# Block 2's attention: unscaled probabilities, and outputs divided by row sums that a transpose spreads

## The chip, the cores and the metric

One NeuronCore of a Trainium2 chip runs the whole program. The metric is the device time of one execution in microseconds (us); lower is better.

## What is computed

The program is two transformer blocks over 256 tokens of width 1024, in float32. Only the attention of block 2 is touched here. It has two kinds of eight heads each, head size 64: a windowed attention with a sink (kind 0, four query heads share a key head) and a neighbourhood attention with a bias (kind 1). Cut to what matters:

```python
s = concat([s_loc, s_ctx, sink_col], -1)     # kind 0; kind 1: concat([s_loc + bias, s_ctx], -1)
p = softmax(s, -1)
o = p_loc @ v_loc + p_ctx @ v_ctx            # 512 keys per query
merged = concat([rms_norm(o_a, g_a), rms_norm(o_b, g_b)], -1) @ w_out
x = x + g1 * merged
```

The gated feed-forward network (FFN) of block 2 follows on `x`.

## The kernel before

The attention works in 16 *units* (`typ`, `m`, `qt`): kind, pair of heads, half of the tokens (128 queries). Eight units of kind 0 come first, then eight of kind 1; here they are u0 to u15. Two units with the same `typ` and `m` (u0 and u1, u2 and u3, ...) make a *pair*. Four functions make up a unit:

- `scores` (L1605 to L1648): for each of the two heads, TensorE (PE) writes 128x512 scores into one PSUM bank (`sc`, tag `big`, 4 buffers). VectorE (DVE) takes the row maximum (L1621), or for kind 1 adds the bias and takes the maximum in one instruction (L1628); ScalarE (ACT) takes the exponential and sums it along the row (L1636); DVE forms the reciprocal of the two sums (L1640, 128x2); and the probabilities are scaled by it, the first head's on ACT (L1645), the second head's on DVE (L1647), as the table `NSC = ("AD",)` says.
- `turn` (L1650): PE transposes the probabilities in 128x128 pieces into PSUM (`ptp`, tag `tr`, 2 buffers); ACT copies one head's to SBUF, DVE the other's (`pT`, L1658).
- `outputs` (L1662): PE multiplies them with the values. The two heads' outputs lie in one tile with 64 rows each, transposed (rows are head dimensions, columns are queries): `po`, 128x256 for a pair, tag `mo`, one buffer.
- `finish` (L1673), once per pair: ACT squares `po` (`osq`, L1676), PE sums the squares down the rows (`psq`, tag `sm`, one buffer), DVE copies the sums (`ssab`, L1680), and ACT and DVE split `po` times the gain into a high and a low part (`moh` L1681, `mol` L1682). After a kind's fourth pair the rstd of the RMS norm is formed.

Then the output projection: 48 matmuls into four banks `pqa` (kind 0) and 48 into four banks `pqb` (kind 1), 128x512 each, in three terms (`moh`, `mol` with `wq..h`, `wq..l`). DVE evicts each bank with rstd and gate (`tmp` L1747, `tmpb` L1757) and POOL or DVE adds it to `x` (L1748, L1759, L1761). DVE also splits the weights (`wq0l` to `wq3l`, and `fg0l` for the FFN; L196), ACT makes their high parts (L189).

The code issues a unit's scores one unit ahead (`AHEAD = 1`) and a pair's `finish` after the next unit has begun (`LATE`). The order in which each engine really runs its instructions is not that of the code: the program is built with `schedule_with_timeline_sim=True`, which rearranges all of them ahead of time. At run time each engine takes its own list strictly in order and waits where an operand isn't there.

Of the kernel before, what the change touches and what calls it, by code (L numbers as in the profile page):

```python
# [12 lines left out]
AF = mybir.ActivationFunctionType  # L13
ALU = mybir.AluOpType
# [3 lines left out]
P = 128  # L18
# [91 lines left out]
def tile_kernel(ctx: ExitStack, tc: tile.TileContext, I, out, dbg=None):  # L110
    nc = tc.nc
    PE, ACT, DVE, POOL, SP = Ordered(tc, nc.tensor), nc.scalar, nc.vector, nc.gpsimd, nc.sync
# [20 lines left out]
    def at(shape, tag, name, bufs=1, dt=F32):  # L133
        return S_["act"].tile(shape, dt, tag=tag, name=name, bufs=bufs)
# [15 lines left out]
    def pt_(shape, tag, name):  # L150
        return S_["ps"].tile(shape, F32, tag=tag, name=name, bufs=S_["banks"][tag])

    def psm(shape, name, tag="sm"):
        return pso.tile(shape, F32, tag=tag, name=name)
# [62 lines left out]
    def rstd_of(ssq, n, mean, eps, name):  # L217

        v = tmp_([P, n], "rv", name + "v", bufs=4)
        DVE.tensor_scalar(v, ssq, mean, eps, op0=ALU.mult, op1=ALU.add)  # L220
        r = tmp_([P, n], "rs", name, bufs=4)
        S_["pow"] = POOL.tensor_tensor(r, v, mhalf[:, :n], op=ALU.pow)
        return r
# [58 lines left out]
    ident = cst[:, C_ID:C_ID + P]  # L282
# [441 lines left out]
    for tt in range(2):  # L724
        p = pt_([P, 4, P], "rec", "po")
# [73 lines left out]
    prs = {}  # L799
# [83 lines left out]
    for tt in range(2):  # L883
        ts = slice(tt * P, (tt + 1) * P)
        for i in range(2):
            p = pt_([P, 4, P], ("gu", "y")[tt], "pt")
# [406 lines left out]
    for u in range(8):  # L1293
# [85 lines left out]
        p = pt_([P, 256], "tr", "pst")  # L1379
# [163 lines left out]
    def proj_lat(c0, name):  # L1543
        hi, lo = latw[c0]
        if c0 in NEXT:
            n = NEXT[c0]
            latw[n] = split_w(kvw[n], "lat", pool=PLAT)
        p = pt_([P, 2, 256], "big", name + "p")
        for tt in range(2):
            ts = slice(tt * P, (tt + 1) * P)  # L1550
            for k in range(8):
                mm3(p[:, tt], hth[:, k, ts], htl[:, k, ts], hi[:, k], lo[:, k], k == 0, k == 7)
        return p
# [19 lines left out]
    for n, (c0, name, use) in enumerate(jobs):  # L1573
        if n == 3:
            after(ACT.activation(ready, mhalf[:, :1], AF.Exp), S_["hi"])
        p = proj_lat(c0, name)
# [25 lines left out]
    rab = []  # L1602
    ssab = at([P, 2, 2, 4], "ssab", "ssab")

    def scores(typ, m, qt):  # L1605

        q = (qa, qb)[typ]
        ts = slice(qt * P, (qt + 1) * P)
        t_ = at([P, 4, 2], "st", "st", bufs=4)
        scs = [pt_([P, 2, 256], "big", "sc2") for _ in range(2)]  # L1610
        for s in (1, 0):
            for s_ in range(2):
                kh, kl = (kAa[s][:, m // 2], kLa[s][:, m // 2]) if typ == 0 else (kAb[s][:, s_, m], kLb[s][:, s_, m])
                PE.matmul(scs[s_][:, s], lhsT=q[:, s_, m, ts], rhs=kh, start=True, stop=False)
                PE.matmul(scs[s_][:, s], lhsT=q[:, s_, m, ts], rhs=kl, start=False, stop=s + typ >= 1)
        prs = [at([P, 2, 256], "prb2", "prb2", bufs=NPR) for _ in range(2)]
        for s_ in range(2):
            sc = scs[s_]
            if typ == 0:
                PE.matmul(sc[:, 0, (1 - qt) * P:(2 - qt) * P], lhsT=identb, rhs=(maskc, maskn)[qt], start=False, stop=True)  # L1620
                DVE.tensor_reduce(t_[:, 0, s_:s_ + 1], sc, axis=AX.XY, op=ALU.max)  # L1621
            else:

                h = 2 * m + s_
                o = h % 4 * 384 + (2 - 2 * qt) * 64
                w = biasT[h][:, o:o + 256]
                w = bass.AP(tensor=w.tensor, offset=w.offset, ap=[w.ap[0], [1536 - o, 2], [1, 256]])
                DVE.tensor_tensor_reduce(prs[s_], sc, w, 1.0, NEG, ALU.add, ALU.max, t_[:, 0, s_:s_ + 1])  # L1628
        if typ == 0:
            DVE.scalar_tensor_tensor(t_[:, 0], t_[:, 0], -0.125, nsink[:, 2 * m:2 * m + 2], op0=ALU.mult, op1=ALU.min)  # L1630
            DVE.tensor_tensor(t_[:, 3], sinkB[:, 2 * m:2 * m + 2], t_[:, 0], op=ALU.add)
            ACT.activation(t_[:, 3], t_[:, 3], AF.Exp)
        else:
            DVE.tensor_scalar(t_[:, 0], t_[:, 0], -1.0, None, op0=ALU.mult)
        for s_ in range(2):
            S_["exp"] = ACT.activation(prs[s_], prs[s_] if typ else scs[s_], AF.Exp, bias=t_[:, 0, s_:s_ + 1],  # L1636
                                       scale=1.0 if typ else 0.125, accum_out=t_[:, 1, s_:s_ + 1])
        if typ == 0:
            DVE.tensor_tensor(t_[:, 1], t_[:, 1], t_[:, 3], op=ALU.add)
        DVE.reciprocal(t_[:, 2], t_[:, 1])  # L1640
        for s_ in range(2):
            r_ = t_[:, 2, s_:s_ + 1]
            e = NSC[(8 * typ + 2 * m + qt) % len(NSC)][s_]
            if e == "A":
                ACT.activation(prs[s_], prs[s_], AF.Copy, scale=r_)  # L1645
            else:
                (POOL if e == "P" else DVE).tensor_scalar(prs[s_], prs[s_], r_, None, op0=ALU.mult)  # L1647
        return prs,  # L1648

    def turn(prs):  # L1650
        pTs = []
        for s_ in range(2):
            pt = pt_([P, 4, P], "tr", "ptp")
            pf = prs[s_].rearrange("p s (a b) -> p (s a) b", b=P)
            for j in range(4):
                PE.transpose(pt[:, j], pf[:, j], ident)
            pT = at([P, 4, P], "pT2", "pT2", bufs=NPT)
            (DVE.tensor_copy if s_ else ACT.copy)(pT, pt)  # L1658
            pTs.append(pT)
        return pTs  # L1660

    def outputs(typ, m, qt, po_, pTs):  # L1662
        ts = slice(qt * P, (qt + 1) * P)
        for j in range(4):
            for s_ in range(2):
                h = 2 * m + s_
                if typ == 0:
                    v_ = va[j // 2][:, j % 2, (m // 2) * 64:(m // 2) * 64 + 64]
                else:
                    v_ = vb[j // 2][:, j % 2, h * 64:h * 64 + 64]  # L1670
                PE.matmul(po_[64 * s_:64 * s_ + 64, ts], lhsT=v_, rhs=pTs[s_][:, j], start=j == 0, stop=j == 3)

    def finish(typ, m, po_):  # L1673
        k = 4 * typ + m
        osq = at([P, 256], "mt", "osq2", bufs=3)
        ACT.activation(osq, po_, AF.Square)  # L1676
        psq = psm([P, 2], "psq")
        for tt in range(2):
            PE.matmul(psq[:, tt:tt + 1], lhsT=osq[:, tt * P:(tt + 1) * P], rhs=ones1, start=True, stop=True)
        DVE.tensor_copy(ssab[:, typ, :, m], psq)  # L1680
        ACT.activation(moh[:, k], po_, AF.Copy, scale=onT[:, k:k + 1])  # L1681
        DVE.scalar_tensor_tensor(mol[:, k], po_, onT[:, k:k + 1], moh[:, k], op0=ALU.mult, op1=ALU.subtract)  # L1682
        if m == 3:
            ssum = at([P, 2], "ssum", "ssum", bufs=2)
            DVE.tensor_reduce(ssum, ssab[:, typ], axis=AX.X, op=ALU.add)
            rab.append(rstd_of(ssum, 2, 1.0 / 512, EPS, f"rab{typ}"))
# [6 lines left out]

    units = [(typ, m, qt) for typ in range(2) for m in range(4) for qt in range(2)]
    ahead_ = [scores(*units[i]) for i in range(AHEAD)]
    late = []

    def hooks(i):

        nonlocal g1B  # L1700
        if i in G1U:
            g1B = row_bc(mod[:, 2, :, 0], kvc.tile([P, D], F32, tag="fB", name="g1B"))
        for h in BMU.get(i, ()):
            bias_mask(h)
        if i in WQU:
            w_blk2[WQU.index(i)] = w_block(WQU.index(i))
            after(S_["hi0"], S_["exp"])
# [4 lines left out]
    for i, un in enumerate(units):  # L1712
        pTs = turn(*ahead_.pop(0)) if AHEAD == 2 else None
        if late:
            finish(*late.pop())
        if i + AHEAD < len(units):
            ahead_.append(scores(*units[i + AHEAD]))
        pTs = pTs or turn(*ahead_.pop(0))
        if un[2] == 0:
            po_ = psm([P, 256], "po", "mo")  # L1720
        outputs(*un, po_, pTs)
        hooks(i)
        if un[2] == 1:
            late.append((*un[:2], po_))
            if not LATE:
                finish(*late.pop())
    PE.stop()
    if late:
        finish(*late.pop())
# [152 lines left out]
MBN = "wk1"  # L1882
WARM = 16
WK1 = True
NSC = ("AD",)
NSM = "DD"
JKA = (True, True)
RBH = True
# [30 lines left out]
```

## Time and profile before

| what | us |
|---|---|
| median of 3 runs | 825.78 (825.03 to 829.31) |
| the profiled execution, its own time | 826.81 |
| its span, first to last instruction | 825.0 |
| attention and output projection of block 2 (first score matmul to last add to `x`) | 523.2 to 618.9 |
| FFN of block 2 | 618.9 to the end |

The profiled execution is 1.0 us above the median, and 1.8 us of its time lie outside the span. PE is the busiest engine over the whole program, and the chain that ends last lies on it for most of the FFN; a matmul's end is modelled, so PE shown as 100% busy isn't PE at its limit. In the listed stretches busy time is to be compared with the length of the stretch, engine by engine.

### The profile page before, as it was taken

To read this page: it belongs to the slowest core of one execution; us is meant where nothing else is said; L and a number is where in the kernel's file an instruction comes from. 1 tells how busy PE (TensorE), PEld (TensorE's weight loads), DVE (VectorE), ACT (ScalarE), POOL (GpSimd) and SP (SyncE) were. 2 spreads that over 40 slices of the span, in tenths; PEclk is the share of its full clock that TensorE was granted. 3 is DMA by queue.
4 is the path that set the end of the run, shared out by engine and by line. 5 is a ranking of instruction groups with operands and counts; after the bars stand their busy time and mean duration, and the time that the engine had idled before them with its cause. 6 is when DMAs were issued, how large, how long until landed. Compare 5 with 4: busy or idle time off the path is not lost. (4 is left out here: it accounts for less than half of the span.)

```text
span 825.0 us, 14982 instructions
## 1 busy us (share of the span) xinstructions
PE 748.6 (91%) x6244; PEld 601.9 (73%) x6244; DVE 424.9 (52%) x954; ACT 302.3 (37%) x533; POOL 108.5 (13%) x96
## 2 busy tenths in 40 slices
PE   7999999999789978588788999698988999999997
PEld 7887887966644435275554889687867999999996
DVE  4767543475712214103223789878655554555545
ACT  5532233453420010001113663498725343443441
POOL 5011000053000000000000476400122000000000
PEclk9999999999899999899889999899998999999999
DMA  7999878568489999999998505111542665565201
GB/s 213 356 386 391 288 278 304 219 262 351 185 340 419 420 417 419 408 405 409 410 398 294 155 20 166 45 53 52 158 149 94 215 203 174 184 200 169 92 1 52
DMA packets 87590, 201.15 MB, mean 244 GB/s; under 512 B 15496, under 2 KB 63040, under 8 KB 75232
## 3 DMA queue, kind: packets, MB, share of 16 engines
q1 hardware_dynamic: 87328, 200.06, 66.0%
q8 instruction: 50, 0.82, 0.4%
q0 software_dynamic: 192, 0.11, 0.1%
q14 instruction: 20, 0.16, 0.1%
HBM read 199.21 MB, written 1.05 MB: 243 GB/s over the span
## 5 line engine op out<-in xcount | busy, mean ns | idle before, releaser
L103 PE MATMUL pfu<-hif,fuh 128*128 128x256 f32 x176 | 50.4, 286 | 1.6 <-ACT fuh L189 1.6
L103 PE MATMUL pfu<-hif,ful 128*128 128x256 f32 x176 | 50.3, 286 | 0.8 <-POOL ful L196 0.8
L103 PE MATMUL pfu<-lof,fuh 128*128 128x256 f32 x176 | 50.3, 286 | 0.0
L103 PE MATMUL pyd<-ed,hid 128*32 128x512 f32 x256 | 40.1, 663 | 8.3 <-DMA ed<-in_w_down_dram 3.6
L103 PE MATMUL pfg<-hif,fgh 128*128 128x256 f32 x160 | 45.5, 284 | 0.0
L103 PE MATMUL pfg<-lof,fgh 128*128 128x256 f32 x160 | 45.5, 284 | 0.0
L103 PE MATMUL pfg<-hif,fgl 128*128 128x256 f32 x160 | 45.4, 284 | 0.0
L196 DVE TENSOR_TENSOR fdl<-fd,fdh 128x512 fp32r<-128x512 f32 x44 | 27.5, 686 | 28.7 <-ACT fdh L189 28.7
L1384 ACT ACTIVATE sg<-pgu,r1s 128x256 f32<-128x256 f32 x8 | 3.8, 474 | 92.6 <-PE pgu L103 68.8
L103 PE MATMUL pgu<-eg,xg 128*32 128x256 f32 x512 | 35.4, 397 | 1.8 <-DVE sg L1385 1.1
L103 PE MATMUL pgu<-eu,xg 128*32 128x256 f32 x512 | 34.6, 396 | 2.0 <-DMA eu<-in_w_up_dram 2.0
L1411 DVE TENSOR_TENSOR yl<-pyd,yh 128x512 fp32r<-128x512 f32 x16 | 11.1, 691 | 48.6 <-ACT yh L1410 36.8
L189 ACT ACTIVATE fuh<-fu 128x1024 fp32r<-128x1024 f32 x22 | 22.1, 1053 | 36.8 <-issue 28.6
L103 PEld LDWEIGHTS pfu<-hif,fuh 128*128 128x128 f32 x176 | 34.2, 194 | 1.8 <-ACT fuh L189 1.8
L189 ACT ACTIVATE fdh<-fd 128x1024 fp32r<-128x1024 f32 x22 | 22.1, 1051 | 36.7 <-issue 35.8
L103 PE MATMUL pf<-fdl,fh 128*128 128x512 f32 x88 | 35.1, 399 | 0.0
L103 PEld LDWEIGHTS pfu<-hif,ful 128*128 128x128 f32 x176 | 34.2, 194 | 1.1 <-POOL ful L196 1.1
L103 PE MATMUL pf<-fdh,fh 128*128 128x512 f32 x88 | 34.7, 394 | 0.0
L103 PEld LDWEIGHTS pfu<-lof,fuh 128*128 128x128 f32 x176 | 34.3, 195 | 0.0
L103 PE MATMUL pf<-fdh,fl 128*128 128x512 f32 x88 | 34.0, 392 | 0.0
L103 PEld LDWEIGHTS pyd<-ed,hid 128*32 128x32 f32 x256 | 9.5, 118 | 32.1 <-issue 21.5
L196 DVE TENSOR_TENSOR fgl<-fg,fgh 128x512 fp32r<-128x512 f32 x40 | 27.7, 754 | 9.3 <-ACT fgh L189 9.3
(721 smaller groups left out, 2168.7 us busy)
## 6 DMA issues: line engine op xcount, KB each, us to landing
eg<-in_w_gate_dram SPq DMA_DIRECT2D x32, 1024.0 KB, 17.4
eu<-in_w_up_dram SPq DMA_DIRECT2D x32, 1024.0 KB, 19.6
ed<-in_w_down_dram SPq DMA_DIRECT2D x32, 1024.0 KB, 15.4
wmod<-in_w_mod_dram SPq DMA_DIRECT2D x24, 1024.0 KB, 10.5
fg<-in_w_gate_dram SPq DMA_DIRECT2D x11, 1024.0 KB, 5.6
fu<-in_w_up_dram SPq DMA_DIRECT2D x11, 1024.0 KB, 5.7
fd<-in_w_down_dram SPq DMA_DIRECT2D x11, 1024.0 KB, 5.0
kv<-in_w_in_dram SPq DMA_DIRECT2D x5, 1024.0 KB, 15.3
```

What stands on the lines that cost most here:

```text
L103: return self._keep(self.engine.matmul(*args, **kwargs))
L189: S_["hi"] = ACT.activation(hf[:, s], vf[:, s], AF.Copy)
L196: i = (POOL if c in pool else DVE).tensor_tensor(lf[:, s], vf[:, s], hf[:, s], op=ALU.subtract)
L1384: ACT.activation(sg, pgu[:, 0], AF.Silu, scale=r1s[:, u:u + 1])
L1411: DVE.tensor_tensor(yl, py, yh, op=ALU.subtract)
```

## The change

The probabilities stay unscaled. Per unit, DVE now forms the reciprocals with each of the two sums repeated 64 times, 128x128 values (`rr`, 3 buffers), and PE transposes that tile: each row of the result belongs to one output dimension of one of the two heads, each column to a query, as in `po`. It lands in a tile `rows` of 128x258 in PSUM (tag `sm`, one buffer per pair), whose last two columns take the place of `psq`. In `finish`, ACT copies the 128x256 rows to SBUF (`on_`, which shares the two buffers of tag `qn_`), and DVE multiplies `po` by them; `osq`, `moh` and `mol` then read the product in SBUF instead of `po`. The scaling on ACT and DVE (16 + 16 instructions) goes, and so does the table `NSC`.

```diff
 # scores
-        DVE.reciprocal(t_[:, 2], t_[:, 1])
-        for s_ in range(2):
-            r_ = t_[:, 2, s_:s_ + 1]
-            e = NSC[(8 * typ + 2 * m + qt) % len(NSC)][s_]
-            if e == "A":
-                ACT.activation(prs[s_], prs[s_], AF.Copy, scale=r_)
-            else:
-                (POOL if e == "P" else DVE).tensor_scalar(prs[s_], prs[s_], r_, None, op0=ALU.mult)
+        rr = at([P, 2, 64], "rr", "rr", bufs=3)
+        DVE.reciprocal(rr, bc(t_[:, 1], 64))
+        sums[typ, m, qt] = rr.rearrange("p a b -> p (a b)")
         return prs,
 # outputs
         ts = slice(qt * P, (qt + 1) * P)
+        PE.transpose(rows_[typ, m][:, ts], sums[typ, m, qt], ident)
 # finish
         k = 4 * typ + m
+
+        on_ = at([P, 2, 256], "qn_", "on_", bufs=2)
+        ACT.activation(on_[:, 0], rows_[typ, m][:, 0:256], AF.Copy)
+        DVE.tensor_tensor(on_[:, 1], po_, on_[:, 0], op=ALU.mult)
+        po_ = on_[:, 1]
         osq = at([P, 256], "mt", "osq2", bufs=3)
         ACT.activation(osq, po_, AF.Square)
-        psq = psm([P, 2], "psq")
+        psq = rows_[typ, m][:, 256:258]
 # loop over the units
             po_ = psm([P, 256], "po", "mo")
+            rows_[un[:2]] = psm([P, 258], "rows")
```

The lists of all engines are rearranged with it. Three places matter here.

VectorE, just ahead of the output projection. Before (`fg0l` is the FFN's first weight; pT_5727 belongs to u10, pT_5778 to u11):

```order
L1647 TENSOR_SCALAR prb_5757<-prb_5757,st 128x512
L1658 COPY pT_5727<-ptp 128x512
L196 TENSOR_TENSOR wq1l<-wq_5789,wq1h 128x512 x2
L196 TENSOR_TENSOR fg0l<-fg,fg0h 128x512 x2
L1628 ISA prb_5861,st<-sc_5851,bias_5149 128x512
L1628 ISA st 128x1
L1658 COPY pT_5778<-ptp 128x512
```

And now (pT_5738 belongs to u9):

```order
L196 TENSOR_TENSOR wq1l<-wq_5804,wq1h 128x512 x2
L1636 TENSOR_SCALAR st<-st 128x2
L1676 TENSOR_TENSOR on__5635<-po,on__5635 128x256
L1630 ISA prb_5878,st<-sc_5868,bias_5151 128x512
L1630 ISA st 128x1
L196 TENSOR_TENSOR fg0l<-fg,fg0h 128x512 x4
L1685 SCALAR_TENSOR_TENSOR mol<-on__5635,onT,moh 128x256
L1655 COPY pT_5738<-ptp 128x512
```

All four pieces of `fg0l` now stand ahead of the copy of u9, where u11's copy followed two of them.

PE, from the last value matmuls ahead of the projection to the first `pqa`. Before (pT_5778 is u11, prb_5810 is u12):

```order
L103 MATMUL po<-pT_5778,vb_3522 64x128
L103 MATMUL po<-pT_5825,mixed 64x128
L106 MATMUL ptp<-cst,prb_5810 128x128 x4
L103 MATMUL pqa_6029<-wq0h,moh 128x512
L103 MATMUL pqa_6029<-wq0l,moh 128x512
```

And now (prb_5825 is u12):

```order
L103 MATMUL po<-pT_5738,vb_3522 64x128
L106 MATMUL ptp<-cst,prb_5770 128x128 x4
L106 MATMUL rows<-cst,rr 128x128 x2
L103 MATMUL sc_5967<-kAb_3523,qb 128x256
L103 MATMUL sc_5967<-kLb_3524,qb 128x256
L103 MATMUL sc_5967<-kAb_4478,qb 128x256
L103 MATMUL sc_5967<-kLb_4438,qb 128x256
L106 MATMUL ptp<-cst,prb_5771 128x128 x4
L106 MATMUL ptp<-cst,prb_5825 128x128 x4
L103 MATMUL pqa_6053<-wq0h,moh 128x512
```

The projection begins after the same unit's transposes (u12), but the value matmuls of u10 and u11 now come behind its start.

PE, the end of the projection. Before, the four banks end together:

```order
L103 MATMUL pqb_6092<-wq3l,moh 128x512
L103 MATMUL pqb_6089<-wq3h,mol 128x512
L103 MATMUL pqb_6090<-wq3h,mol 128x512
L103 MATMUL pqb_6091<-wq3h,mol 128x512
L103 MATMUL pqb_6092<-wq3h,mol 128x512
L106 MATMUL pt<-cst,x 128x128 x16
```

Now three banks end (6113 to 6115), and the fourth's twelve matmuls follow, of which the first three and the last stand here:

```order
L103 MATMUL pqb_6113<-wq3h,mol 128x512
L103 MATMUL pqb_6114<-wq3h,mol 128x512
L103 MATMUL pqb_6115<-wq3h,mol 128x512
L103 MATMUL pqb_6116<-wq2h,moh 128x512
L103 MATMUL pqb_6116<-wq2l,moh 128x512
L103 MATMUL pqb_6116<-wq2h,mol 128x512
...
L103 MATMUL pqb_6116<-wq3h,mol 128x512
L106 MATMUL pt<-cst,x 128x128 x16
```

`pt` are the transposes of the finished `x` with which the FFN begins.

## Rows read from the trace of the kernel before

**Rows 1.** The page: part 1, busy time; part 4, the chain by engine.

```profile
PE 748.6 (91%) x6244; PEld 601.9 (73%) x6244; DVE 424.9 (52%) x954; ACT 302.3 (37%) x533; POOL 108.5 (13%) x96
...
PE 27%; DVE 2%; POOL 0%; ACT 0%; issue 0%; DVEq 0%
```

**Rows 2.** The two stretches: us, busy us per engine (instructions), clock, DMA share, GB/s.

```profile
523.00:581.00 58.00, 52.13 (x460) 45.57 (x461) 48.88 (x140) 46.74 (x109) 3.45 (x4) 0.94 0.13 38
581.00:618.00 37.00, 33.72 (x219) 26.95 (x218) 21.16 (x44) 15.86 (x32) 8.91 (x7) 1.00 0.53 169
```

**Rows 3.** The chain in order of time, 579 to 615: start, us, what.

```profile
581.40 4.79 PE pqa L103 x21
...
592.59 0.44 PE ptp L106 x4
...
604.65 0.34 PE psq L103 x4
...
606.49 1.02 PE po L103 x16
...
612.15 2.21 PE pqb L103 x9
```

**Rows 4.** VectorE groups by line and shape: total us, mean ns | idle before.

```profile
L1658 DVE COPY pT<-ptp 128x512 f32<-128x512 f32 x16 | 11.0, 688 | 10.0 <-PE ptp L106 8.9 <-PE po L103 0.9
...
L1647 DVE TENSOR_SCALAR prb<-prb,st 128x512 f32<-128x512 f32 x16 | 7.7, 483 | 0.2
...
L1682 DVE SCALAR_TENSOR_TENSOR mol<-po,onT,moh 128x256 fp32r<-128x256 f32 x8 | 3.8, 474 | 5.2 <-ACT moh L1681 5.2
...
L1640 DVE RECIPROCAL st<-st 128x2 f32<-128x2 f32 x16 | 2.6, 160 | 3.1 <-ACT prb L1636 3.0
...
L819 DVE RECIPROCAL mst<-mst 128x4 f32<-128x4 f32 x4 | 0.7, 174 | 0.1
...
L501 DVE RECIPROCAL gy<-gy 128x8 f32<-128x8 f32 x1 | 0.2, 195 | 0.0
...
L377 DVE RECIPROCAL sc2t<-sc2t 128x16 f32<-128x16 f32 x1 | 0.2, 240 | 0.0
...
L1628 DVE CUSTOM_DVE_ANT_1 prb<-sc,bias 128x512 f32<-128x512 f32 x14 | 9.5, 682 | 0.3 <-PE ptp L106 0.3
```

**Rows 5.** Tile view of the probabilities, one VectorE line: ns min/median/max.

```profile
L827 DVE TENSOR_SCALAR prb<-prb,mst x16: 273/344/1370, 176.0 to 198.1; 128x128 f32<-128x128 f32 x8, 128x256 f32<-128x256 f32 x8
```

**Rows 6.** Groups by line and shape on ScalarE.

```profile
L1645 ACT ACTIVATE prb<-prb,st 128x512 f32<-128x512 f32 x16 | 11.5, 720 | 0.7 <-DVE st L1640 0.7
L1676 ACT ACTIVATE osq<-po 128x256 f32<-128x256 f32 x8 | 3.1, 384 | 12.8 <-PE po L103 12.8
```

**Rows 7.** Four single microseconds, columns as in rows 2.

```profile
521.00:522.00 1.00, 0.00 (x0) 0.00 (x0) 1.00 (x1) 0.00 (x0) 1.00 (x2) 1.00 0.00 0
...
524.00:525.00 1.00, 1.00 (x6) 0.99 (x5) 0.97 (x2) 0.00 (x0) 1.00 (x2) 0.50 0.00 0
...
616.00:617.00 1.00, 0.00 (x0) 0.00 (x0) 1.00 (x2) 0.42 (x1) 1.00 (x2) 1.00 0.00 0
...
620.00:621.00 1.00, 0.98 (x6) 0.58 (x4) 0.13 (x1) 0.00 (x0) 0.71 (x1) 0.50 0.00 0
```

**Rows 8.** The timeline from 611 to 621: start, us, engine, line.

```profile
611.11 0.38 ACT L1676 ACTIVATE osq<-po 128x256 f32<-128x256 f32 x1 [8.57 <-PE po L103]
...
614.45 2.73 DVE L1757 SCALAR_TENSOR_TENSOR tmpb<-pqb,rab,g1B 128x512 f32<-128x512 f32 x4 [1.60 <-PE pqb L103]
...
615.28 2.49 POOL L1759 TENSOR_TENSOR x<-tmpb,x 128x512 f32<-128x512 f32 x2 [1.58 <-DVE tmpb L1757]
...
617.09 1.83 DVE L1761 TENSOR_TENSOR x<-x,tmpb 128x512 f32<-128x512 f32 x2
...
620.97 1.23 PE L103 MATMUL rpf<-cst,rf 128*128 128x128 f32 x4
```

More of the change, by code (lines that the diff above doesn't have):

```diff
@@ L1603, in tile_kernel @@
     ssab = at([P, 2, 2, 4], "ssab", "ssab")
+    sums, rows_ = {}, {}
     def scores(typ, m, qt):
@@ L1884 @@
 WK1 = True
-NSC = ("AD",)
 NSM = "DD"
```

## The prediction, made before the changed kernel ran

> **What bounds the kernel now.** I read the page first, for the engine that the whole program waits on: PE is busy for 91% of the span, but that number counts overlapping matmuls; the chain that ended last names PE for 27% of the span, nearly all of it in the FFN, and DVE for 2% [rows 1]. The FFN comes behind the change and isn't touched, so the change is worth what it moves the start of the FFN by. Next, busy time by stretch [rows 2]: from 523 to 581 us, where the scores, the softmax and most of the value matmuls lie, DVE is busy for 48.9 of 58 us, ACT for 46.7; from 581 to 618, the output projection, DVE only for 21.2 of 37 and ACT for 15.9. So the first stretch goes at the pace of DVE and ACT, with DVE ahead of ACT by a little, and the second at that of PE: its chain is PE from 581.40 to 614.36 without a longer break [rows 3]. The views by line then give the prices [rows 4 to 6], and the timeline the end [rows 8].
>
> **What goes and what comes, on each engine.** *ACT* loses 16 scalings of 0.720 us, 11.5 us, and gains 8 copies of 128x256 out of PSUM, priced like its square of the same shape, 0.384 each, 3.1 us [rows 6]: 8.4 us less. ACT isn't the fuller of the two, so this counts only through what waits for it. *DVE* loses 16 scalings of 0.483 (7.7 us) and 16 reciprocals of two columns at 0.160 (2.6) [rows 4]. It gains 8 products of 128x256 with one operand in PSUM, priced like `mol`, 0.474 each (3.8), and 16 reciprocals of 128 columns, which the trace doesn't show. It has them at 2, 4, 8 and 16 columns: 160, 174, 195 and 240 ns [rows 4]. That is some 150 ns fixed and 5.7 ns a column (80 ns over 14 columns), so 128 columns cost 0.160 + 126 x 0.0057 = 0.88 us. The bounds: no less than another DVE instruction of 128 columns, 0.273 [rows 5]; no more than the steepest step, 7 ns a column from 2 to 4, which gives 1.04. I take 0.88, as the four rows lie on one line. DVE thus gains 14.1 + 3.8 and loses 10.3: 7.6 us more on the fuller engine. That speaks against the change, although 32 instructions of 512 columns go. *PE* gets 16 transposes, 0.11 each by the group of four in 0.44 [rows 3], 1.8 us in all.
>
> The Trainium skill ("VectorE: DVE Perf Modes", section "Walkthrough: the 8-slice pipeline in each mode") says that the reciprocal is an iterated division with a repeat count of 8. If that is eight clocks of its 0.96 GHz for each element, it would be 8.3 ns a column and about 1.2 us for 128, as an estimate from that page; the slope in this trace is 5.7 ns, so the page read in this way isn't borne out here, and the sum would come out about 4 us longer by it.
>
> **First stretch.** What counts is when PE can start `pqa`. In the new order PE waits ahead of it for DVE's copy pT_5738. Up to there DVE has, against the 48.9 us before the old start [rows 2]: 13 scalings (6.3) and 13 small reciprocals (2.1) fewer, 11 large ones more (9.7), 4 products more (1.9), 3 bias instructions of 0.68 (2.0), one copy of 0.69 and one `mol` of 0.47 fewer, since fewer units are done by then. That is 48.9 us: no more work, but less far on. In the old run DVE stood idle for 9.1 us in this stretch; 8.9 us of such waits, over the whole attention, were copies waiting for PE's transposes [rows 4], and those now come sooner, as nothing lies between exponential and transpose. Against that stand new waits: with three buffers for `rr`, a unit's reciprocal must wait until PE has transposed that of three units earlier. I let the idle time fall by 2 us; the bounds are no fall and 4 us. Then the copy ends at 523 + 48.9 + 7.1 = 579.0. PE follows with four groups of transposes at 0.44, 7/8 of a unit's value matmuls (1.02 a unit), two single transposes and four score matmuls priced as one more group [rows 3], 3.3 us in all: `pqa` starts at 582.3 instead of 581.40, **0.9 us later**.
>
> **Second stretch.** From that start to the last `pqb` PE took 33.0 us. Now two and an eighth units of value matmuls more lie behind it (2.2 us), six of the new transposes (0.66) and one more `psq` at 0.34 [rows 3]: **3.2 us more**. The lists also put new waits here. `pqb` needs the split of `wq2` and `wq3`, which follow the last exponentials on ACT, and these hang on DVE, where the reciprocal for u13 stands ahead of them and waits for a transpose that PE issues only after 31 of the `pqa` matmuls. And the value matmuls of u14 need `po` back, which the product of the pair before frees, behind four splits of `wq3` on DVE. The margins at these places, worked out with the prices above, are within 2 us of zero. I take **1.0 us**; the bounds are 0 and 4.
>
> **The end.** Before, all four `pqb` banks end within the last four matmuls, and behind them lie four evictions (2.73 us) and two additions on DVE (1.83), until 618.92 [rows 8], 4.5 us after the last matmul. Now three banks end twelve matmuls earlier, 12 x 0.228 = 2.7 us (4.79 us for 21) [rows 3], in which their evictions, POOL's two additions (2.49) and one of DVE's fit; behind the last matmul are one eviction (0.68) and one addition (0.92), and some 0.2 of waits: **2.7 us less**. The new tail of `finish` for the last pair (a copy on ACT, 0.38, and the product, 0.47, ahead of the square) lies beside nine `pqb` matmuls of 2.05 us and I price it at nothing; without that cover it would be 0.9.
>
> **Sum:** 0.9 + 3.2 + 1.0 - 2.7 = +2.4 us. The profiled execution took 826.81 us, 1.0 above the median, and would be 829.2; on the median of 825.78 this is **828.2 us**. A difference of 0.5%, 4.1 us, is about what a measurement of this kernel can tell from no change, so this is "the same".
>
> **Rivals.** *DVE is the bound and gives nothing back.* Its idle time doesn't fall (2.0 us), a reciprocal costs 1.04 (11 x 0.16 = 1.8), and PE, which waits for pT_5738 with nothing else to issue, stands long enough for the clock to go down. Twice in the old trace PE stood: at 521 and at 616 it does nothing, and at 524 and 620 the granted clock is 0.50, the 1.2 GHz level [rows 7]; about 3.4 us at half speed cost 1.7. Together 828.2 + 5.5 = 833.7, slower. For it: DVE has 7.6 us more to do and is full already. Against it: the idle time is mostly waiting for PE, which gets its input earlier. It decides once pT_5738 ends later than about 580.5. By the Trainium skill's page above, taken as eight clocks a column, this case would be about 2 us longer still.
>
> *The reciprocal is as cheap as other DVE instructions*, 0.273 [rows 5]. Eleven of them save 6.7 us ahead of the projection, and the new waits of 1.0 behind it go too: 828.2 - 7.7 = 820.5, faster. For it: ACT's 8.4 us would then count in full. Against it: four rows on one line with a slope that no other DVE instruction has (0.688 us for 512 columns is 1.3 ns a column).
>
> *The change moves nothing.* Work goes from ACT to DVE and PE, the lists absorb it, and the new end balances the backlog: 825.8. I count it with the forecast, since both are the same to a measurement.
>
> **How the numbers follow.** Forecast with the third rival 0.51; DVE-bound 0.36; cheap reciprocal 0.13. The forecast's own range is 824 to 831: 2 us either way for the idle time, 1 down and 3 up for the waits. The low end for all, 820.5, is the cheap reciprocal; the high end, 834.5, takes in the DVE-bound case and a little of the bound of 4 us on the waits. Forecast and third rival lie within 0.5% (821.65 to 829.91), up to 0.02 above it; the dear case is slower. So faster 0.13, same 0.49, slower 0.38.
>
> **What would show each step.** The line of the reciprocal: 16 instructions of about 0.88 us; 0.3 or 1.04 would move it to a rival. The busy time of DVE in its first 58 us above that of ACT by more than 10 us. `pqa` starting within 2 us of 581.4. In the timeline, three `tmpb` evictions before the last `pqb` matmul, and the transposes of `x` within 2 us of that matmul. The forecast is wrong if the order's end doesn't give its 2.7 us back, or if PE stands in the projection for more than about 4 us (a reciprocal on DVE ahead of the last bias instruction would be what it stands behind).

## The result and the profile after

The changed kernel takes **834.89 us** (median of 11 runs, 830.92 to 837.62); the kernel before, run beside it, 827.62 (11 runs, 825.03 to 831.72). The ratio is **1.0074, 95% interval 1.0054 to 1.0095**: 6.1 us slower, 4.5 to 7.9 by the interval, and all of it above the half per cent that counted as no change. (The two medians alone differ by 7.3 us; where kernels are compared below, it is by their ratios to the kernel before.) On the median of 825.78 that the prediction started from, this is 831.9, between the forecast (828.2) and the rival in which DVE is the bound (833.7).

The page of the changed kernel, parts 1 and 4, against [rows 1]:

```profile
PE 754.0 (91%) x6260; PEld 606.2 (73%) x6260; DVE 432.8 (52%) x946; ACT 295.4 (35%) x525; POOL 107.9 (13%) x96
...
PE 25%; DVE 3%; ACT 1%; issue 1%; POOL 0%; DVEq 0%; POOLq 0%; ACTq 0%
```

PE is busy 5.4 us longer, with 16 instructions more; DVE 7.9 us longer; ACT 6.9 us shorter. The two stretches of [rows 2], the same columns:

```profile
523.00:581.00 58.00, 50.18 (x430) 44.17 (x431) 51.74 (x124) 38.04 (x94) 5.08 (x5) 0.90 0.11 37
581.00:618.00 37.00, 33.91 (x240) 26.96 (x237) 22.18 (x42) 16.69 (x35) 4.01 (x3) 0.97 0.46 148
```

DVE is busy for 51.7 of the first 58 us and ACT for 38.0, where they stood at 48.9 and 46.7, and the clock in the first stretch is 0.90 instead of 0.94. These are fixed times, though, and the changed run has its first score matmul at 524.91, 1.74 us later than before (523.17), in a part that nobody touched. So I cut both runs at events of the attention: from the first score matmul to the first `pqa`, from there to the end of the last `pqb`, and from there to the first matmul of `rpf`, which opens the FFN. Windows of the kernel before, columns as in rows 2:

```profile
523.17:581.15 57.98, 52.28 (x462) 45.71 (x463) 48.89 (x141) 46.90 (x109) 3.28 (x4) 0.94 0.13 39
581.15:615.02 33.87, 33.40 (x217) 26.62 (x215) 18.04 (x38) 14.79 (x28) 6.42 (x5) 1.00 0.56 179
615.02:620.97 5.95, 3.13 (x17) 2.54 (x17) 4.93 (x10) 2.06 (x6) 3.20 (x3) 0.83 0.10 32
```

and of the changed kernel:

```profile
524.91:584.36 59.45, 53.54 (x450) 47.20 (x451) 51.95 (x126) 40.38 (x99) 3.17 (x4) 0.89 0.10 36
584.36:623.80 39.44, 36.35 (x245) 28.43 (x243) 24.66 (x47) 14.59 (x29) 7.27 (x7) 1.00 0.50 161
623.80:629.04 5.24, 3.14 (x16) 2.36 (x17) 4.18 (x7) 2.06 (x6) 1.97 (x3) 0.85 0.01 3
```

The three pieces are 1.47 and 5.57 us longer and 0.71 shorter: **+6.3 us**. Behind `rpf` both runs take the same 204.0 us. In the middle piece PE works 2.95 us more and stands 3.09 us instead of 0.47. These are the waits of PE in that piece:

```profile
PE po L103 <- DVE on__5955 L1676: 2.3, 1, 2.3
PE pqb L103 <- DVE wq2l L196: 0.7, 1, 0.7
```

The groups by line and shape on DVE, against [rows 4]:

```profile
L1643 DVE RECIPROCAL rr<-st 128x128 f32<-128x128 f32 x16 | 14.6, 933 | 5.1 <-PE rows L106 5.1
...
L1655 DVE COPY pT<-ptp 128x512 f32<-128x512 f32 x16 | 10.8, 676 | 2.0 <-PE po L103 2.0
```

The wide reciprocal takes 0.933 us, the product about 0.4 (0.36 to 0.43), and the copies of the transposes now wait for PE 2.0 us in all instead of 10.0.

**Ahead of `pqa`.** PE's timeline (start, us, what; in brackets the idle time before it and what ended it):

```profile
572.38 0.70 PE L106 MATMUL ptp<-cst,prb 128*128 128x128 f32 x4 [1.90 <-ACT pT L1655]
...
574.76 1.12 PE L103 MATMUL po<-pT,mixed 128*64 128x128 f32 x8 [0.82 <-DVE on__5635 L1676]
...
578.82 1.09 PE L106 MATMUL ptp<-cst,prb 128*128 128x128 f32 x4
...
583.57 1.03 PE L106 MATMUL ptp<-cst,prb 128*128 128x128 f32 x8
584.36 0.48 PE L103 MATMUL pqa<-wq0h,moh 128*128 128x512 f32 x1
```

and two windows over the same place:

```profile
570.00:573.00 3.00, 1.10 (x9) 0.90 (x9) 3.00 (x6) 2.76 (x8) 0.00 (x0) 0.98 0.67 231
573.00:583.00 10.00, 9.18 (x56) 7.89 (x55) 7.78 (x21) 6.06 (x14) 0.71 (x1) 0.50 0.00 0
```

The second of them in the kernel before:

```profile
573.00:583.00 10.00, 8.32 (x72) 7.04 (x73) 9.78 (x27) 9.49 (x20) 0.01 (x1) 1.00 0.26 78
```

PE stands for 1.90 and 0.82 us, is busy for 1.10 of the 3 us from 570 on, and from 573 to 583 its granted clock is 0.50, the 1.2 GHz level. The four transposes at 578.82 take 1.09 us, as long as the eight at 583.57 behind that stretch (1.03). PE is busy for 9.18 of the 10 us, so it hardly stands there, it is slow. In the kernel before the clock is 1.00 in the same ten microseconds.

**Behind `pqa`.** DVE's timeline:

```profile
593.79 1.76 DVE L1643 RECIPROCAL rr<-st 128x128 f32<-128x128 f32 x2 [4.48 <-PE rows L106]
595.47 0.36 DVE L1676 TENSOR_TENSOR on__5857<-po,on__5857 128x256 f32<-128x256 f32 x1
...
596.35 0.68 DVE L1630 CUSTOM_DVE_ANT_1 prb<-sc,bias 128x512 f32<-128x512 f32 x1
...
598.12 1.24 DVE L1636 TENSOR_SCALAR st<-st 128x2 f32<-128x2 f32 x1
...
603.88 1.29 DVE L196 TENSOR_TENSOR wq2l<-wq,wq2h 128x512 fp32r<-128x512 f32 x2 [3.86 <-ACT wq2h L189]
...
608.87 2.48 DVE L196 TENSOR_TENSOR wq3l<-wq,wq3h 128x512 fp32r<-128x512 f32 x4
611.28 0.41 DVE L1676 TENSOR_TENSOR on__5955<-po,on__5955 128x256 f32<-128x256 f32 x1
```

DVE stands for 4.48 us ahead of the two reciprocals for u13 and u14: they want buffers of `rr` that PE reads only at 593.48, behind 31 `pqa` matmuls. Behind them in DVE's list stands the last bias add (596.35), behind that, on ACT, the last exponentials and the first copy of `wq2` (602.79, before at 592.58), and behind that the splits (603.88) and the product that frees `po` (611.28), for which PE stands 2.3 us.

The 4.48 us are not what the buffers cost. The next instruction in DVE's list is the product `on__5857`, and it needs all value matmuls of u10 and u11. PE's timeline:

```profile
593.48 0.38 PE L106 MATMUL rows<-cst,rr 128*128 128x128 f32 x2
...
594.18 0.70 PE L103 MATMUL po<-pT,vb 128*64 128x128 f32 x7
```

The last of these matmuls end at 594.88. With buffers to spare DVE would have stood for the product instead, until at most 0.6 us before the product did run. Matmuls and transposes both stand behind the 31 `pqa` matmuls in PE's list, so in these lists it is their order, more than the ring of buffers, that holds DVE here. A further 1.1 us of the chain lie at 598.12: the negation of two columns of maxima, for which the last exponentials wait, takes 1.24 us instead of 0.16, beside an addition of POOL (597.89 to 599.34).

**The end.** All engines:

```profile
616.02 0.44 PE L106 MATMUL rows<-cst,rr 128*128 128x128 f32 x2
...
616.98 0.42 DVE L1676 TENSOR_TENSOR on__6033<-po,on__6033 128x256 f32<-128x256 f32 x1 [2.54 <-ACT on__6033 L1675]
...
619.51 1.30 POOL L1752 TENSOR_TENSOR x<-tmp,x 128x512 f32<-128x512 f32 x1 [3.72 <-DVE ssab L1683]
...
619.73 1.10 DVE L220 TENSOR_SCALAR rab1v<-ssum 128x2 f32<-128x2 f32 x1
...
620.97 0.71 POOL L222 TENSOR_TENSOR rab<-rab1v,mhalf 128x2 f32<-128x2 f32 x1 [0.17 <-DVE rab1v L220]
...
621.71 2.07 DVE L1761 SCALAR_TENSOR_TENSOR tmpb<-pqb,rab,g1B 128x512 f32<-128x512 f32 x3 [0.89 <-POOL rab L222]
...
623.41 0.39 PE L103 MATMUL pqb<-wq3h,mol 128*128 128x512 f32 x1
623.82 1.79 DVE L1765 TENSOR_TENSOR x<-x,tmpb 128x512 f32<-128x512 f32 x1
...
625.53 0.74 DVE L1761 SCALAR_TENSOR_TENSOR tmpb<-pqb,rab,g1B 128x512 f32<-128x512 f32 x1
...
629.04 1.22 PE L103 MATMUL rpf<-cst,rf 128*128 128x128 f32 x4 [0.27 <-POOL rf L222]
```

The last pair's sums are turned at 616.02, `rab` is there at 621.68, and only then do three evictions run, 2.1 us before PE's last `pqb` ends at 623.80. DVE's first addition takes 1.79 us and stands ahead of the fourth eviction, which starts 1.73 us after PE has ended.

### The profile page after: what moved, and what is told of

Same layout as the page of the kernel before. It is cut to its first block, busy times and chain, and to the rows that moved or that the text cites. A ratio compares the mean times of both kernels' runs of the same rounds, so it can differ in the third digit from the quotient of the medians.

```text
span 833.1 us, 15007 instructions
## 1 busy us (share of the span) xinstructions
PE 754.0 (91%) x6260; PEld 606.2 (73%) x6260; DVE 432.8 (52%) x946; ACT 295.4 (35%) x525; POOL 107.9 (13%) x96
## 5 line engine op out<-in xcount | busy, mean ns | idle before, releaser
L1411 DVE TENSOR_TENSOR yl<-pyd,yh 128x512 fp32r<-128x512 f32 x16 | 11.1, 691 | 47.1 <-ACT yh L1410 35.3
L103 PE MATMUL pgu<-eu,xg 128*32 128x256 f32 x512 | 32.5, 380 | 1.9 <-DMA eu<-in_w_up_dram 1.9
```

Source lines behind the costliest of these rows:

```text
L103: return self._keep(self.engine.matmul(*args, **kwargs))
L1411: DVE.tensor_tensor(yl, py, yh, op=ALU.subtract)
```

## The experiments

Three theories. **A, the price:** 16 reciprocals of 0.93 us fill DVE's list until the projection waits for it. **B, the wait:** reciprocals that wait for a buffer of `rr` hold up all that stands behind them. **C, the order:** every edit makes new lists, and any new list moves the time by some us. Each kernel ran for five rounds beside the kernel before, 12 runs in all (e6 and e10: 6, e9: 5), in four groups on four chips: e1 to e4, e5 to e7, e8 to e10, e11 and e12. Pieces are from one profiled execution each, cut as above. How far one execution can be trusted shows ahead of the attention, where PE, DVE and ACT run the same lists in all kernels: up to the first score matmul thirteen of the fourteen executions take 522.8 to 525.5 us, and that of e10, the slowest of its six runs, 529.3. The sums of e6 and e11, the same kernel, differ by 0.5.

| Kernel | ratio to before, 95% | to `pqa` | to last `pqb` | to `rpf` | sum |
|---|---|---|---|---|---|
| before | 1 | 57.98 | 33.87 | 5.95 | 97.80 |
| changed | 1.0074 [1.0054, 1.0095] | 59.45 | 39.44 | 5.24 | 104.13 |
| e1 no scaling | 0.9964 [0.9950, 0.9978] | 55.51 | 33.56 | 5.95 | 95.02 |
| e2 wide reciprocal, unread | 0.9955 [0.9937, 0.9973] | 52.28 | 36.24 | 5.95 | 94.47 |
| e3 other order | 0.9995 [0.9973, 1.0017] | 57.72 | 35.34 | 6.08 | 99.14 |
| e4 POOL spreads | 1.0010 [0.9991, 1.0030] | 55.84 | 36.89 | 6.25 | 98.98 |
| e5 wide, six buffers | 1.0017 [0.9997, 1.0037] | 56.41 | 38.23 | 5.24 | 99.88 |
| e6 narrow, three buffers | 0.9946 [0.9927, 0.9965] | 51.93 | 37.39 | 5.55 | 94.87 |
| e7 ACT spreads, late | 0.9992 [0.9973, 1.0011] | 54.05 | 38.15 | 5.26 | 97.46 |
| e8 narrow, six buffers | 0.9993 [0.9979, 1.0006] | 52.15 | 38.31 | 5.52 | 95.98 |
| e9 wide twice, six buffers | 1.0158 [1.0137, 1.0179] | 65.75 | 38.44 | 5.93 | 110.12 |
| e10 wide, two buffers | 1.0065 [1.0045, 1.0084] | 58.63 | 39.23 | 6.13 | 103.99 |
| e11 = e6 again | 0.9938 [0.9915, 0.9961] | 51.46 | 37.36 | 5.52 | 94.34 |
| e12 narrow, two buffers | 0.9962 [0.9940, 0.9984] | 51.72 | 37.53 | 5.50 | 94.75 |

**e1, the gain without the cost.**

```diff
-        for s_ in range(2):
-            r_ = t_[:, 2, s_:s_ + 1]
...
-                ACT.activation(prs[s_], prs[s_], AF.Copy, scale=r_)
...
-                (POOL if e == "P" else DVE).tensor_scalar(prs[s_], prs[s_], r_, None, op0=ALU.mult)
```

> The kernel before with the 32 scalings of the probabilities left out and nothing in their place (the outputs of the attention stay undivided): the gain of the change without its cost. 8.4 us of ACT and 7.7 us of DVE work go; PE's work is the same. Theory A (the price of the wide reciprocal on the fuller queue decides): both queues become slack, TensorE's 5.7 us of idle time and low clock between the first score matmul and the first pqa matmul shrink, 2 to 4 us faster than before. Theory B (the loss is in waits that the order of the lists makes, most of it behind the first pqa matmul): TensorE stays the bound, 0 to 1.5 us faster. Theory C (any other order of the lists moves the time by some us): anything within 3 us, without relation to the work removed.

Measured 825.35 us against 828.46, 3.0 us faster. That is A's size. The first two windows:

```profile
523.25:578.76 55.51, 52.11 (x462) 45.62 (x462) 44.51 (x132) 40.83 (x99) 3.16 (x4) 0.94 0.13 40
578.76:612.32 33.56, 33.08 (x215) 26.50 (x214) 15.31 (x31) 11.63 (x22) 6.13 (x5) 1.00 0.58 182
```

2.5 us come ahead of `pqa`, where DVE has 4.4 us less to do. Leaving out the 32 scalings is worth about 3 us.

**e2, the price alone.**

```diff
-        DVE.reciprocal(t_[:, 2], t_[:, 1])
+        rr = at([P, 2, 64], "rr", "rr", bufs=3)
+        DVE.reciprocal(rr, bc(t_[:, 1], 64))
```

(on e1)

> The kernel before without the scalings (left out) and with the 16 reciprocals of 128 columns, whose results nobody reads: no transpose, no copy, no product, no wait for a buffer of theirs. DVE does 14.9 - 2.6 - 7.7 = 4.6 us more than before, ACT 8.4 us less. Theory A: the stretch up to the first pqa matmul is 1 to 2 us longer than before, the whole 1 to 2.5 us slower than before and 3 to 6 us slower than the kernel without scalings alone. Theory B: within 1 us of the kernel without scalings alone. Theory C: no relation.

Measured 824.64 us, 3.8 faster than before and 0.7 faster than e1. A expected a loss; B's number holds.

```profile
524.04:576.32 52.28, 48.34 (x440) 42.47 (x441) 47.84 (x118) 37.43 (x92) 3.47 (x4) 0.97 0.12 41
576.32:612.56 36.24, 35.68 (x238) 27.82 (x237) 23.32 (x45) 14.57 (x29) 6.62 (x5) 1.00 0.53 171
```

DVE is busy for 47.8 of 52.3 us, so the reciprocals go into time in which it stood. What nobody reads holds nobody up.

**e3, another order.**

```diff
-NSC = ("AD",)
+NSC = ("DA",)
```

(on the kernel before)

> The kernel before with the two engines of the scalings exchanged (of each pair of heads the first on DVE, the second on ACT): the same work on each engine, and other lists. Theories A and B: within 1 us of the kernel before, since no wait is added and no queue gets fuller. Theory C: 2 us or more to either side, in lists that carry the same work; then a loss of 6 us may be half of that kind.

Measured 828.31 us against 828.46: nothing. C isn't seen here.

**e4, POOL spreads.**

```diff
-        DVE.reciprocal(rr, bc(t_[:, 1], 64))
+        DVE.reciprocal(t_[:, 2], t_[:, 1])
+        POOL.tensor_copy(rr, bc(t_[:, 2], 64))
```

> The changed kernel with the reciprocal of two columns on DVE and its spreading over 128 columns by a copy on POOL, in the same place of the program: 16 x (0.93 - 0.16) = 12.3 us leave DVE, and the wait for one of the three spread buffers stands in POOL's list instead of DVE's. Theory A: the stretch up to the first pqa matmul gets back its 1.5 us or more, and the last bias add no longer waits behind that buffer: 3 to 5 us faster than the changed kernel. Theory B: the first stretch stays as in the changed kernel within 0.5 us, only the wait behind the buffer goes: 2 to 3 us faster, all of it behind the first pqa matmul. Theory C: no relation. A fourth reading, in which the chain of the last pair (spread rows, product, square, sums, rab) sets the end alone: within 1 us of the changed kernel.

Measured 828.70 us against 828.46: 5.3 us of the 6.1 are back, a little more than A's 3 to 5, and both pieces took part.

```profile
524.08:579.92 55.84, 50.24 (x451) 43.80 (x451) 45.02 (x128) 39.32 (x95) 7.62 (x16) 0.97 0.12 39
579.92:616.81 36.89, 36.88 (x242) 28.80 (x242) 20.02 (x45) 16.16 (x33) 7.34 (x9) 1.00 0.54 171
```

The piece to `pqa` is 3.6 us shorter than in the changed kernel, at a clock of 0.97, and PE no longer stands in the second (36.88 of 36.89 us). This takes price and wait off DVE together, so it doesn't tell them apart. POOL's copy takes 0.307 us:

```profile
L1644 POOL COPY rr<-st 128x128 f32<-128x128 f32 x16 | 4.8, 307 | 59.0 <-PE rows L106 30.0 <-DVE st L1643 10.7 <-DVE st L1636 7.9
```

**e5, the wait taken away and the price kept.**

```diff
-        rr = at([P, 2, 64], "rr", "rr", bufs=3)
+        if qt == 0:
+            k = 4 * typ + m
+            pair_[typ, m] = at([P, 2, 2, 64], "rB", "rr2") if k % 3 == 2 else at([P, 2, 2, 64], "rr", "rr", bufs=2)
+        rr = pair_[typ, m][:, qt]
         DVE.reciprocal(rr, bc(t_[:, 1], 64))
```

> The changed kernel with room for the spread sums of six units instead of three (one tile for a pair of units, two of them in a tag of their own and every third pair in the free tile of the row scale rB): the 16 reciprocals of 128 columns stay on DVE, at 0.93 us each, and no reciprocal waits for PE to have read an older one. Theory B (the wait, not the price): the 2.6 us that TensorE idles behind the first pqa matmul go, and the last bias add, the copies of the third and fourth block of weights and the last pair move up with them: 2.5 to 5 us faster than the changed kernel, nearly the time of the kernel with POOL's spreading. Theory A (the price of the wide reciprocal in the full queue and the low clock behind it): the stretch up to the first pqa matmul stays 1.5 us longer than before; 0 to 1.5 us faster than the changed kernel.

Measured 829.74 us against 828.70; by the ratios 4.7 us faster than the changed kernel, and the two intervals don't touch. That is inside B's 2.5 to 5. A's 0 to 1.5 is wrong, and so is its longer first stretch: the piece to `pqa` takes 56.41 us, before 57.98. The reciprocals are as dear as ever and wait for PE no more:

```profile
L1646 DVE RECIPROCAL rr<-st 128x128 f32<-128x128 f32 x16 | 15.0, 944 | 2.2 <-ACT prb L1638 2.2
```

```profile
522.80:579.21 56.41, 51.27 (x451) 44.36 (x451) 51.42 (x124) 38.59 (x95) 2.46 (x3) 0.95 0.11 39
579.21:617.44 38.23, 36.77 (x242) 28.48 (x242) 25.20 (x49) 16.16 (x33) 8.18 (x8) 1.00 0.51 165
```

PE stands for 1.46 instead of 3.09 us behind `pqa`, and that piece is 1.2 us shorter. But B's way there isn't borne out: 3.0 of the 4.2 us in the pieces lie ahead of `pqa`, where the changed kernel's reciprocals wait for a buffer for only 0.59 us. There the same 450 matmuls take 51.3 instead of 53.5 us, at a clock of 0.95 instead of 0.89: 2.3 of the 3.0. And the last bias add hardly moves up. It starts 11.40 us after the first `pqa`, in the changed kernel 11.99:

```profile
590.60 0.68 DVE L1630 CUSTOM_DVE_ANT_1 prb<-sc,bias 128x512 f32<-128x512 f32 x1
```

With the buffers the lists of PE, DVE and ACT have changed too, ahead of `pqa` and behind it, so C is in this comparison as well.

**e6, a narrow reciprocal, both on DVE.**

```diff
-        DVE.reciprocal(rr, bc(t_[:, 1], 64))
+        DVE.reciprocal(t_[:, 2], t_[:, 1])
+        DVE.tensor_copy(rr, bc(t_[:, 2], 64))
```

> The changed kernel with the reciprocal of two columns and a copy that spreads it over 128 columns, both on DVE: by the rows of a 128x128 copy and of a two-column reciprocal some 0.16 + 0.27 instead of 0.93 us, 8 us less in all, and the three buffers and their wait stay on DVE. Theory B: within 1.5 us of the changed kernel, as long as a copy still waits for its buffer ahead of the last bias add or of the copies of the weights. Theory A: 3 us or more faster than the changed kernel.

Measured 824.33 us against 828.70: 4.5 us faster than before. That is A's direction, but it doesn't refute B, since the condition set for B isn't met: in the new list the two copies stand behind the last bias add, and hardly wait.

```profile
L1644 DVE COPY rr<-st 128x128 f32<-128x128 f32 x16 | 4.1, 264 | 0.2 <-PE rows L106 0.2
```

```profile
523.27:575.20 51.93, 49.60 (x446) 43.81 (x447) 41.41 (x131) 37.01 (x90) 3.16 (x4) 0.95 0.13 42
575.20:612.59 37.39, 36.75 (x248) 28.82 (x246) 25.48 (x58) 18.11 (x39) 6.74 (x6) 1.00 0.54 169
```

**e7, ACT spreads, where the transpose stands.**

```diff
-        rr = at([P, 2, 64], "rr", "rr", bufs=3)
-        DVE.reciprocal(rr, bc(t_[:, 1], 64))
-        sums[typ, m, qt] = rr.rearrange("p a b -> p (a b)")
+        DVE.reciprocal(t_[:, 2], t_[:, 1])
+        sums[typ, m, qt] = t_
...
+        rr = at([P, 2, 64], "rr", "rr", bufs=3)
+        ACT.copy(rr, bc(sums[typ, m, qt][:, 2], 64))
+        PE.transpose(rows_[typ, m][:, ts], rr.rearrange("p a b -> p (a b)"), ident)
```

> The changed kernel with the reciprocal of two columns on DVE, kept in six small tiles, and its spreading over 128 columns by a copy on ACT, asked for only where the unit's transpose stands: neither the price nor the wait is left on DVE; ACT does some 16 x 0.3 = 5 us more and is still 3 us below before. Theories A and B alike: the time of the kernel with POOL's spreading or better (within 1 us of the kernel before, down to 2 us faster than it). Theory C, in which the end is set by the last pair's chain alone: as the changed kernel.

Measured 827.55 us against 828.70: as the kernel before, as A and B said; the reading by which the last pair's chain sets the end alone is wrong.

**e8, neither price nor wait, with the buffers of e5.** e5 with the two lines of e6.

> The kernel with room for six units' spread sums, and the reciprocal of two columns with a spreading copy on DVE instead of the reciprocal of 128 columns (0.16 + 0.26 for 0.94 us, 8 us of DVE work less). If the price of the wide reciprocal is what is left of the loss once the wait is gone (the full queue up to the first pqa matmul), it comes out where the narrow reciprocal with three buffers did, 5 us faster than with the wide one: 4 to 5 us faster than before. If the narrow kernel with three buffers only had a lucky list, this one stands with the other kernels that have neither price nor wait on DVE (POOL's and ACT's spreading): within 1.5 us of before.

Measured 826.84 us against 827.27: with e4 and e7, not with e6. Against e5 only 2.0 us, and the two intervals overlap. Its windows:

```profile
525.53:577.68 52.15, 49.04 (x447) 43.19 (x448) 41.41 (x131) 37.05 (x90) 3.16 (x4) 0.97 0.13 42
577.68:615.99 38.31, 36.94 (x248) 28.75 (x246) 26.09 (x58) 18.02 (x39) 7.21 (x6) 1.00 0.52 165
```

The piece to `pqa` is 4.3 us shorter than e5's, for 10.0 us less DVE work, and the three pieces together 3.9; the ratios show half of that.

**e9, the price twice.** e5 with its line of the reciprocal doubled.

> The kernel with room for six units' spread sums, and every wide reciprocal done twice into the same tile: 16 x 0.94 = 15 us more DVE work, and no wait for a buffer. If the price in the queue counts, at the rate of the step from narrow to wide (8 us of DVE work for some 5 us), it is 6 to 10 us slower than with one, 7 to 11 us slower than before. If the price alone is covered (as the wide reciprocals that nobody reads were), within 2 us of the kernel with one.

Measured 839.79 us against 827.27; 11.7 us slower than e5 by the ratios, beyond what was expected for a price that counts.

```profile
524.49:590.24 65.75, 52.77 (x450) 45.71 (x451) 62.53 (x141) 39.43 (x96) 2.50 (x4) 0.92 0.10 33
590.24:628.68 38.44, 38.43 (x243) 29.61 (x242) 24.66 (x46) 15.71 (x33) 6.66 (x6) 0.96 0.51 164
```

DVE is busy for 62.5 of 65.8 us ahead of `pqa`: 11.1 us more work than in e5 made that piece 9.3 us longer. In e5 DVE still stood for 5.0 us, here for 3.2. One wide reciprocal for each unit leaves DVE's list near the brim, and a second runs over.

**e10, two buffers.** The changed kernel with `bufs=2` for `rr`.

> The changed kernel with two buffers for the spread sums instead of three: the price stays, more reciprocals wait for PE to have read an older one, two of them ahead of the last bias add and two ahead of the copies of the fourth block of weights. If the wait counts: at least as slow as the changed kernel, and up to 4 us slower, with the time in the waits of DVE's reciprocals for PE's row transposes. If it is the price alone: within 1 us of the changed kernel.

Measured 832.69 us against 827.27, 0.7 below the changed kernel by the ratios: no loss beyond three buffers. DVE's reciprocals wait for PE 5.0 us, as long as in the changed kernel (5.1):

```profile
DVE rr L1643 <- PE rows L106: 5.0, 2, 2.6
```

The expectation held at neither's expense: "at least as slow" and "within 1 us" both fit.

**e11 and e12, the fastest form again, and with two buffers.** e6 unchanged; e6 with `bufs=2`.

> The narrow reciprocal and the spreading copy on DVE with three buffers, once more and on another chip, beside the two-buffer form of it: if its 4.5 us below the kernel before belong to the kernel, the ratio comes out between 0.993 and 0.9965 again; if they were that chip's or those runs', it comes out with the form for six units, at 0.998 to 1.0005.

> The same with two buffers for the spread sums. With a short copy in the list the wait stands behind the last bias add, not ahead of it: if the place of the wait decides what it costs, within 1.5 us of the form with three buffers. If fewer buffers cost by themselves (as six against three did with the wide reciprocal, 4.7 us), 2 us or more slower than it.

Measured 823.97 and 825.92 us against 828.91: 0.62% and 0.38% faster than before. The gain of e6 belongs to the kernel. Two buffers come out 2.0 us behind three with overlapping intervals, between the two readings, so this one is undecided; in the pieces they differ by 0.4 us.

**What follows.** Two kernels have 5 us of DVE's reciprocals waiting for PE, the changed one and e10, and lose 6.1 and 5.4 us. In the others DVE waits for PE with `rr` for 1.1 us at most, and all of them but e9 lie at 1.0017 or below. e5 has the price without the wait and loses 1.4, not told apart from zero, so the price of the 16 reciprocals by itself doesn't make the loss. That the wait makes it isn't shown. By the trace the buffers cost at most 0.6 us at the 4.48 us wait, most of what e5 wins back lies ahead of `pqa`, and its lists are others. So 4.7 of the 6.1 us go away with three more buffers, through the wait or through the lists that come with them; which of the two stays open.

The price of the wide reciprocal is near the brim: nothing in e2, about 2 us from e8 to e5 (their intervals overlap), 11.7 from e5 to e9. With neither price nor wait, the change costs nothing (e4, e7, e8) or gains 4.5 to 5.1 us (e6, e11), which makes e6 a version that beats both kernels, by some 11 us the changed one.

Two more things stay open. Between e6 and e8, which do the same work with three and with six buffers, lie 4 us, nearly as much as between the changed kernel and e5, and here six buffers are the slower ones. Up to `pqa` PE and ACT run the same lists in both. Of the 4.3 us between the two profiled executions the pieces show 1.1; 2.3 lie ahead of the first score matmul and 0.9 behind the first `rpf`, where both run the same lists on these engines and DVE. So for most of it the order of the lists is no explanation, and no run shows another. Nor is it shown where the 10 us at 0.50 came from, or whether they belong to the kernel. The changed kernel's mean granted clock is 0.964 over its 11 runs and e5's 0.968 over 12, but that of the kernel before goes from 0.967 (the 35 runs beside e1) to 0.963 (the 23 beside e11), and e1 has a clock of 0.50 from 575 to 578 us too, without any of these waits. Among the changed kernel's own runs the two with the highest clock, 0.969, take 830.9 and 833.1 us, the two with the lowest, 0.957 and 0.961, 837.4 and 837.6.

## Why the prediction was right and wrong

- **The reciprocal, 0.88 us:** 0.933. The four narrow rows [rows 4] lie nearly on one line with it: 0.933 - 0.160 over 126 columns is 6.1 ns a column. The Trainium skill ("VectorE: DVE Perf Modes", section "Walkthrough: the 8-slice pipeline in each mode"), read as eight clocks an element, would have given about 1.2 us; the trace doesn't agree with that reading. The cheap rival fell with it, and DVE's total, +7.6 forecast, is +7.9.
- **First stretch, +0.9:** +1.5, for other reasons. The copy pT_5738 was to end 55.8 us after the first score matmul; it ended at 578.72, 53.8 after. But PE then took 5.64 us to `pqa` instead of 3.3, most of them at a granted clock of 0.50.
- **Second stretch, work +3.2:** PE is busy 2.95 us more. **Waits +1.0:** 2.6, at the two places named, the reciprocal for u13 and the product behind the splits of `wq3`. The places were right and the term mis-sized; it was inside its bounds of 0 to 4. What holds DVE at the first place is less the buffer that the prediction named than the product behind it (0.6 us between them).
- **The end, -2.7: the step that failed.** -0.7. The step had three evictions under way while the last twelve matmuls run, which needs `rab` by then, and it priced the last pair's `finish` at nothing. Its copy, product, square, sum and `rab` took 5.7 us, from 616.02 to 621.68, so the evictions had 2.1 us. And the addition, taken as 0.92 [rows 8], took 1.79 ahead of the fourth eviction. Some 0.7 us of the miss is a misreading of the kernel before: 614.36 is where its chain leaves PE, at the first of the four banks to end; the last `pqb` matmul ended at 615.02, so 3.9 and not 4.5 us lay behind it.
- **The sum, +2.4:** +6.3 in the pieces, +6.1 by the ratio. The misses are 0.6, 1.3 (1.6 of waits less 0.3 of work) and 2.0: together 3.9, a third of it the waits, half the end. The forecast's own range of 824 to 831 doesn't follow from the bounds beside it: 2 us either way, 1 down and 3 up around 828.2 give 825.2 to 833.2, and the measured 831.9 lies in that.
- **The rival of a full DVE** came nearest in time, and not by its mechanism. It was to decide once the copy ended 57.3 us or more after the first score matmul; it ended at 53.8. A reciprocal of 1.04 wasn't seen, and DVE's idle time did fall, from 9.1 to 7.5 us. Its half-speed clock came, 10 us long instead of 3.4. That DVE is near the brim is right, by e9; but most of this kernel's loss is gone with DVE's load as it was (e5).

## What to carry to other kernels

A scaling that moves from a wide tile to a narrow one is paid for by what spreads its factor: take the reciprocal of the few numbers and spread them with a copy (0.16 + 0.26 us here) instead of the reciprocal of spread numbers (0.93). When an instruction is put on an in-order engine with a small ring of buffers, find out who frees the buffer and what stands behind the instruction. Then look at what the next instruction in the list waits for before you take the wait for its price: here 4.48 us of waiting for a buffer hid a wait of the next product that would have ended at most 0.6 us earlier. An edit that takes a wait away also makes new lists, so look where the time came back: here most of it came back elsewhere. A gain at a program's end counts only from the last thing that the end needs, here `rab`, and not from the matmuls that finish early.

## What the hardware showed that was not expected

Some DVE instructions that start beside an addition of POOL last until it has ended, and others aren't touched. In the changed kernel `rab1v` (two columns) starts 0.22 us after POOL's addition, takes 1.10 us instead of 0.17 and ends with it; the negated maxima at 598.12 (two columns too) take 1.24 us instead of 0.16 in the same way; the addition of `x` takes 1.79 us beside POOL and 0.69 without. The evictions `tmpb`, which read PSUM, take 0.74 us each beside it and without it, and the reduction ahead of `rab1v` (`ssum`, 0.16 us) isn't slowed by the same addition. The Trainium skill ("GPSIMD Engine Reference", section "Specifications") says that POOL's way into SBUF is shared with VectorE, whose instructions in a 2-port mode or with two SBUF inputs collide there. For the addition, which has two such inputs, the trace agrees; `rab1v` and the negation read one tile, and no run here shows which mode they have. The 0.9 us of `rab1v` lie on the chain to `rab`, the 1.1 us of the negation on the chain to the last exponentials.

POOL's spreading copy of 128x128 (0.307 us) is nearly as fast as DVE's (0.264 on average).
